# Hybrid attention of a two-layer network: heads handled in pairs instead of one by one

## The chip, the cores and the metric

One core of a Trainium2 chip runs the whole program. The metric is the device time of one launch in microseconds (us). The engines are TensorE (PE in the rows, its weight loads PEld), VectorE (DVE), ScalarE (ACT), GpSimd (POOL) and SyncE (SP, which issues the weight loads from memory).

## The reference, cut to what matters

Two blocks run one after the other on a sequence of 256 tokens of width 1024: first a retention layer, a feed-forward, a stick-breaking attention and a mixture of experts, then two layers of a hybrid mixer, each followed by a feed-forward with a convolution. The change lies in the hybrid mixer. Half its width is attention with 8 heads of 64; the three dilated windows act together as one bias over all 256 keys:

```python
q = apply_rotary(heads(aq, ATTN_HEADS))
k = apply_rotary(heads(ak, ATTN_HEADS))
v = heads(av, ATTN_HEADS)
attn = dilated_attention(q, k, v)
...
h_fwd = mlstm_direction(q, k, v, g[0], jax.nn.log_sigmoid(g[1]))
...
mlstm = (hm * mlstm_head_g.astype(f32) * jax.nn.sigmoid(mo.astype(f32))).astype(hn.dtype)
return jnp.concatenate([attn, mlstm], axis=-1) @ w_out
```

The other half is a gated recurrence with 4 heads of 128, forwards and backwards, whose q and k come out of a convolution over 5 tokens and a silu.

## The kernel before, in words

All weights come as units of 128x2048 floats through a ring of buffers (`Stream`). `advance` (L101) splits what has arrived into a high part on ScalarE (`split_h`, L83) and a low part on VectorE (`split_l`, L94), so that a product takes three matmuls of reduced precision. The order of instructions in the program is the order on each engine; nothing reorders them, and a late instruction holds up all behind it on its engine.

`hybrid` walks over 14 units of input weights; unit u ends with an `advance`. Units 0 to 3 give q and k of attention, in halves. `rotated` (L1008) applies the rotation on VectorE into a tile `ro`, `flip` (L1020) turns that tile on TensorE and ScalarE copies it to `qk`. The flip of unit u-1 stands right behind the matmuls of unit u. In unit 3 `gating` (L970) runs a chain of small operations on VectorE. Units 5, 6, 9 and 10 (`projA`) give q and k of the recurrence: `conv` (L1144) on ScalarE, eight `taps` (L1151) on VectorE, a tanh on ScalarE, then `silu` (L1161). Units 4 and 8 give attention's values, units 7 and 11 the recurrence's, units 12 and 13 the output gate.

Units 4 to 12 carry attention, one head a unit: `attend(n)` (L1030) turns the weights of head n-1, multiplies q and k of head n, copies the turned weights, and finds the biased maximum and the exponentials of head n. `normalise(n)` (L1059) follows behind the taps. Two units after the second head of a pair, `pv` (L1065) multiplies with the values. `todo` (L1189) sets where the recurrence stands: `gates` (L1076) computes decay tiles `Dt` (TensorE, then four exponentials on ScalarE), `mscores` (L1099) multiplies them with scores, `mout` (L1112) gives the output of one head.

PSUM has two pools: `psA` (L152), 2 slots of two banks, and `psP` (L155), 4 slots of one bank. A new tile takes the slot that the program has freed longest ago and waits until its last reader is done. `attend` takes one `psA` tile for the turned weights of one head and the scores of the next, `gates` one; each projection, flip, `pv` and `mscores` takes one `psP` tile, `mout` two.

```python
            todo = {1: [(prepare,)], 3: [(gating,)], 5: [(gates, 0)], 6: [(gates, 1)], 7: [(mscores, 0), (mscores, 1)],
                    8: [(mout, 0)], 9: [(gates, 2), (mout, 1)], 10: [(gates, 3)], 11: [(mscores, 2), (mscores, 3)],
                    12: [(mout, 2), (mout, 3)], 13: []}
```

Of the kernel before, what the change touches and what calls it, by code (L numbers as in the profile page):

```python
# [125 lines left out]
def tok(t):  # L126
    return slice(t * 128, t * 128 + 128)
# [6 lines left out]
class Net:  # L134
# [801 lines left out]
    def hybrid(self, l, joint0):  # L936
        nc, tc, a, W = self.nc, self.tc, self.a, self.W
        with tc.tile_pool(name="h1", bufs=1) as p, tc.tile_pool(name="h2", bufs=2) as w:
# [66 lines left out]
            at = p.tile([128, 4, 2, S], F32, tag="at", name="at")  # L1005
            dn = {}

            def rotated(ps):  # L1008

                x = w.tile([128, 2, 4, 2, 32], F32, tag="cv", name="ro")  # L1010
                t1, t2 = (w.tile([128, 2, 8, 32], F32, tag="wk", name=n) for n in ("t1", "t2"))
                for t, i in ((t1, 0), (t2, 1)):
                    nc.vector.tensor_tensor(t, ps.rearrange("p t (h d) -> p t h d", d=32),  # L1013
                                            cs[:, :, i, None, :].to_broadcast([128, 2, 8, 32]), op=OP.mult)
                t1, t2 = (t.rearrange("p t (h i) d -> p t h i d", i=2) for t in (t1, t2))
                nc.vector.tensor_tensor(x[:, :, :, 0, :], t1[:, :, :, 0, :], t2[:, :, :, 1, :], op=OP.subtract)
                nc.vector.tensor_tensor(x[:, :, :, 1, :], t2[:, :, :, 0, :], t1[:, :, :, 1, :], op=OP.add)
                return x.rearrange("p t h i d -> p t (h i d)")
# [8 lines left out]
                else:  # L1027
                    nc.scalar.activation(dst[0], ps, AF.Copy, scale=scale)

            def attend(n):  # L1030

                A = self.psA()
                if n > 0:
                    x = at[:, (n - 1) % 2]
                    for jt in range(2):
                        for it in range(2):
                            nc.tensor.transpose(A[:, 0, jt * S + it * 128:jt * S + it * 128 + 128], x[:, it, tok(jt)],  # L1037
                                                self.ident)
                r = slice(64 * (n % 2), 64 * (n % 2) + 64)
                ps = A[:, 1, :].rearrange("p (t s) -> p t s", t=2)  # L1040
                for t in range(2 if n < 8 else 0):
                    nc.tensor.matmul(ps[:, t, :], lhsT=qk[r, 0, n // 2, tok(t)], rhs=qk[r, 1, n // 2, :],  # L1042
                                     start=True, stop=True)
                if n > 0:
                    nc.scalar.activation(at[:, 2 + (n - 1) % 2], A[:, 0, :].rearrange("p (t s) -> p t s", t=2), AF.Copy)
                if n == 8:
                    return
                x = at[:, n % 2]
                m = self.small(2, "m")
                for t in range(2):  # L1050
                    nc.vector.tensor_tensor_reduce(x[:, t, :], ps[:, t, :], bias[:, t, :], 1.0, -3e38, op0=OP.add,  # L1051
                                                   op1=OP.max, accum_out=m[:, t:t + 1])
                nm = self.small(2, "nm")
                nc.vector.tensor_scalar(nm, m, -1.0, None, op0=OP.mult)
                dn[n] = d = self.small(2, "dn")
                for t in range(2):
                    nc.scalar.activation(x[:, t, :], x[:, t, :], AF.Exp, bias=nm[:, t:t + 1], accum_out=d[:, t:t + 1])

            def normalise(n):  # L1059
                d = dn.pop(n)  # L1060
                nc.vector.reciprocal(d, d)
                x = at[:, n % 2]
                nc.vector.tensor_tensor(x, x, d[:, :, None].to_broadcast([128, 2, S]), op=OP.mult)

            def pv(c):  # L1065
                ps = self.psP([128, S])
# [44 lines left out]

            def mout(h):  # L1112
                x = Dt.pop(h)
                A = [self.psP([128, 2, 129]) for _ in range(2)]

                def o(i, t):
                    return A[i][:, t, :]

                def vv(t):
                    return va[:, t, h, :]  # L1120

                def mm(out, l, r, start, stop):
                    nc.tensor.matmul(out, lhsT=l, rhs=r, start=start, stop=stop)  # L1123

                mm(o(0, 0), x[:, 0, 0:128], vv(0), True, True)
                mm(o(0, 1), x[:, 0, 128:256], vv(0), True, False)
                mm(o(0, 1), x[:, 0, 256:384], vv(1), False, True)
                mm(o(1, 0), x[:, 1, 0:128], vv(0), True, False)
                mm(o(1, 0), x[:, 1, 128:256], vv(1), False, True)
                mm(o(1, 1), x[:, 1, 256:384], vv(1), True, True)  # L1130
                d = self.sm.tile([128, 2, 2], F32, tag="den", name="den")
                for i in range(2):
                    nc.scalar.activation(d[:, i, :], A[i][:, :, 128], AF.Abs)
                    nc.vector.tensor_tensor(d[:, i, :], d[:, i, :], cols[:, 1, :, 32 * i + h], op=OP.max)
                r = self.sm.tile([128, 2, 2], F32, tag="rden", name="rden")
                nc.vector.reciprocal(r, d)
                for t in range(2):
                    y = mix[:, t, tok(h)]
                    nc.vector.tensor_scalar(y, o(0, t)[:, :128], r[:, 0, t:t + 1], None, op0=OP.mult)  # L1139
                    nc.vector.scalar_tensor_tensor(y, o(1, t)[:, :128], r[:, 1, t:t + 1], y, op0=OP.mult, op1=OP.add)  # L1140
                    j = w.tile([128, 128], BF, tag="junk1", name="junk1")
                    nc.scalar.activation(j, y, AF.Square, accum_out=ssq[:, 2 * h + t:2 * h + t + 1])
# [8 lines left out]
            def taps(ps, y, ks, dst):  # L1151
                for j, (o, s) in ((0, (slice(2, S), slice(0, S - 2))), (1, (slice(1, S), slice(0, S - 1))),
                                  (3, (slice(0, S - 1), slice(1, S))), (4, (slice(0, S - 2), slice(2, S)))):
                    for c, k in enumerate(ks):
                        nc.vector.scalar_tensor_tensor(y[:, c, o], ps[:, c, s], k[:, j:j + 1], y[:, c, o],  # L1155
                                                       op0=OP.mult, op1=OP.add)
                th = w.tile([128, 2, S], F32, tag="wk", name="th")
                nc.scalar.activation(th, y, AF.Tanh, scale=0.5)
                return dst, th, y

            def silu(dst, th, y):  # L1161
                nc.vector.scalar_tensor_tensor(dst, th, 1.0, y, op0=OP.add, op1=OP.mult)
# [5 lines left out]
            def mnorm():  # L1168
                nc.scalar.preload_act_table_set("sqrt_and_others")
                nc.scalar.activation(rs, ssq, AF.Sqrt, scale=4.0 / 128, bias=eps4)  # L1170
                nc.vector.reciprocal(rs, rs)
# [20 lines left out]
            for u in range(14):  # L1192
                A = u in (5, 6, 9, 10)
                ps = next(first) if u < 4 else self.projA() if A else self.projB()
                if 0 < u < 5:
                    i = u - 1
                    flip([qk[:, i % 2, i // 2 * 2:i // 2 * 2 + 2]], aq.pop(i), 0, 1.0 if i % 2 else 0.125)
                c = None
                if u < 4:
                    aq[u] = rotated(ps)  # L1200
                elif A:
                    c = conv(ps, (u - 5) % 4, u // 9)
                elif u in (4, 8):
                    i = u // 8
                    nc.scalar.activation(v[:, :, i * 256:i * 256 + 256], ps, AF.Copy)
                elif u in (7, 11):
                    i = u // 11
                    nc.scalar.activation(va[:, :, 2 * i:2 * i + 2, :128], ps.rearrange("p t (h d) -> p t h d", h=2),
                                         AF.Copy)
                else:  # L1210
                    gated(u - 12, ps)
                if u in (7, 9, 11, 13):
                    pv((u - 7) // 2)
                if u == 5:
                    columns()
                if 4 <= u < 13:
                    attend(u - 4)
                if A:
                    c = taps(*c)
                if 4 <= u < 12:  # L1220
                    normalise(u - 4)
                if A:
                    silu(*c)
                if u == 3:
                    W.advance()
                for f in todo.get(u, []):
                    f[0](*f[1:])
                if u == 4:
                    nc.scalar.preload_act_table_set("exp_and_others")
                if u not in (3, 13):  # L1230
                    W.advance()
            mnorm()
            mfinal(0)
            joint = RmsNorm(self, p, w, a["mix_post_g"][l], a["ffn_pre_g"][l], "mqk")
# [325 lines left out]
```

## Time and profile before

| what | value |
|---|---|
| median of 3 runs | 2269.43 us (2269.21 to 2270.16) |
| the profiled execution | 2271.13 us, its span 2269.3 us |
| TensorE busy (matmul) | 2209.9 us, 97% |
| TensorE busy (weight loads) | 1922.5 us, 85% |
| VectorE busy | 1705.9 us, 75% |
| ScalarE busy | 1374.1 us, 61% |
| mean granted clock of TensorE | 0.992 of full |

TensorE is busy for nearly all of the span, the other engines for less; the shares are means over phases with different limits. The two hybrid layers lie at about 1585 to 1702 us and 1930 to 2046 us. A time in a row counts from the start of the span. In a row of a timeline the first number is the start and the second the duration, "x4" counts instructions, and a bracket tells how long the engine sat idle before and what ended that.

### The profile page before, as it was taken

Reading aid. Unit: us, or ns where it says so; the run is one execution under the profiler, and the core shown is the slowest. Engines: PE = TensorE matmul, PEld = TensorE weight load, DVE = VectorE, ACT = ScalarE, POOL = GpSimd, SP = SyncE. Lnnn points to the kernel's source line nnn. Section 1 sums busy time; section 2 is a strip of 40 time slices with the busy share of each in tenths; the row PEclk is TensorE's granted clock in tenths of the full one; section 3 lists DMA queues with packets and bytes.
Section 4 is the critical chain, followed back from the end, with each engine's and each line's share of the span. In section 5 each row is a group of like instructions: output and inputs, shape, how many; then the busy total and the mean of one; then the engine's idle time right before and its main releaser. Section 6 shows DMA issues by size and latency. Waiting matters only on the chain. (4 is left out here: it accounts for less than half of the span.)

```text
span 2269.3 us, 31847 instructions
## 1 busy us (share of the span) xinstructions
PE 2209.9 (97%) x13077; PEld 1922.5 (85%) x13077; DVE 1705.9 (75%) x1671; ACT 1374.1 (61%) x1380; POOL 63.4 (3%) x78
## 2 busy tenths in 40 slices
PE   8999999998999999999999999997999999999998
PEld 8998998987888888878887888886889998888996
DVE  6566554647889888888888888887876975776972
ACT  4353543664777777777776777775556654555752
POOL 4100000010000000000000000000000000000000
PEclk9999999999999999999999999998999999999999
DMA  8444555537988899989998999995234554434551
GB/s 305 163 170 173 200 186 184 174 129 279 397 328 311 303 386 366 352 309 376 355 351 301 345 377 366 353 345 185 94 131 169 205 186 167 151 130 143 204 192 68
DMA packets 80074, 562.07 MB, mean 248 GB/s; under 512 B 9072, under 2 KB 9136, under 8 KB 13488
## 3 DMA queue, kind: packets, MB, share of 16 engines
q1 hardware_dynamic: 76464, 547.39, 65.7%
q0 software_dynamic: 3456, 12.55, 1.7%
q8 instruction: 105, 1.72, 0.3%
q14 instruction: 49, 0.40, 0.0%
HBM read 558.86 MB, written 1.05 MB: 247 GB/s over the span
## 5 line engine op out<-in xcount | busy, mean ns | idle before, releaser
L94 DVE TENSOR_TENSOR wl<-raw,wh 128x2048 fp32r<-128x2048 f32 x518 | 1185.3, 2291 | 318.8 <-ACT wh L83 316.7
L83 ACT ACTIVATE wh<-raw 128x2048 fp32r<-128x2048 f32 x518 | 991.2, 1915 | 393.7 <-PE pp L754 198.7
L200 PE MATMUL pp<-xh,wh 128*128 128x256 f32 x1360 | 389.0, 286 | 7.5 <-ACT wh L194 7.4
L200 PE MATMUL pp<-xh,wl 128*128 128x256 f32 x1360 | 385.6, 283 | 0.1
L200 PE MATMUL pp<-xl,wh 128*128 128x256 f32 x1360 | 384.3, 283 | 0.0
L200 PEld LDWEIGHTS pp<-xh,wh 128*128 128x128 f32 x1360 | 257.0, 189 | 9.3 <-ACT wh L194 8.1
L200 PEld LDWEIGHTS pp<-xl,wh 128*128 128x128 f32 x1360 | 258.8, 190 | 0.5 <-issue 0.5
L200 PEld LDWEIGHTS pp<-xh,wl 128*128 128x128 f32 x1360 | 257.7, 189 | 1.2 <-DVE wl L195 0.9
L200 PE MATMUL pp<-wh,xh 128*128 128x256 f32 x720 | 206.8, 287 | 5.2 <-DVE mix L1139 5.2
L200 PE MATMUL pp<-wh,xl 128*128 128x256 f32 x720 | 203.1, 282 | 0.0
L200 PE MATMUL pp<-wl,xh 128*128 128x256 f32 x720 | 202.6, 281 | 0.0
L754 PE MATMUL pp<-wh,xgh 128*128 128x512 f32 x448 | 179.5, 401 | 3.8 <-DVEq L831 3.8
L754 PE MATMUL pp<-wh,xh 128*128 128x512 f32 x448 | 179.4, 400 | 0.0
L754 PE MATMUL pp<-wl,xgh 128*128 128x512 f32 x448 | 177.2, 396 | 1.5 <-DVE wl L94 1.5
L754 PE MATMUL pp<-wl,xh 128*128 128x512 f32 x448 | 177.7, 397 | 0.7 <-DVE wl L94 0.7
L754 PE MATMUL pp<-wh,xl 128*128 128x512 f32 x448 | 177.6, 396 | 0.0
L754 PE MATMUL pp<-wh,xgl 128*128 128x512 f32 x448 | 177.0, 395 | 0.0
L200 PEld LDWEIGHTS pp<-wh,xh 128*128 128x128 f32 x720 | 136.6, 190 | 7.9 <-issue 6.1
L764 PE MATMUL pa<-wh,hh 128*128 128x512 f32 x448 | 142.0, 398 | 0.7 <-ACT hh L194 0.7
L764 PE MATMUL pa<-wh,hl 128*128 128x512 f32 x448 | 141.4, 397 | 0.0
L764 PE MATMUL pa<-wl,hh 128*128 128x512 f32 x448 | 141.3, 397 | 0.0
L200 PEld LDWEIGHTS pp<-wl,xh 128*128 128x128 f32 x720 | 136.6, 190 | 0.9 <-issue 0.7
(335 smaller groups left out, 3054.4 us busy)
## 6 DMA issues: line engine op xcount, KB each, us to landing
raw<-in_moe_w_in SPq DMA_DIRECT2D x224, 1024.0 KB, 5.4
raw<-in_moe_w_out SPq DMA_DIRECT2D x112, 1024.0 KB, 5.5
raw<-in_w_up SPq DMA_DIRECT2D x44, 1024.0 KB, 4.8
raw<-in_w_in SPq DMA_DIRECT2D x28, 1024.0 KB, 4.8
raw<-in_ret_w_in SPq DMA_DIRECT2D x23, 1024.0 KB, 5.2
raw<-in_ffn_w_in SPq DMA_DIRECT2D x22, 1024.0 KB, 4.8
raw<-in_w_down SPq DMA_DIRECT2D x22, 1024.0 KB, 4.8
raw<-in_ffn_w_out SPq DMA_DIRECT2D x11, 1024.0 KB, 4.8
```

The source lines that it names most:

```text
L83: self.nc.scalar.activation(h, self.rt[i][0], AF.Copy)
L94: self.nc.vector.tensor_tensor(l, r, h.bitcast(F32), op=OP.subtract)
L200: self.nc.tensor.matmul(out, lhsT=w, rhs=x, start=(i == 0), stop=(i == n - 1))
L754: nc.tensor.matmul(q, lhsT=x[:, k, :], rhs=ww[:, kk, :], start=(k == 0 and i == 0), stop=(k == KC - 1 and i == 2))
L764: nc.tensor.matmul(A[0][f], lhsT=x[:, k, :], rhs=ww[:, kk, half(f)], start=(s == 0 and k == 0 and i == 0), stop=(s == SL - 1 and k == 3 an ...
```

## The change

`attend` is split into `scores(c)` and `turn()`, and both work on a pair of heads. In units 4, 6, 8 and 10 `scores` multiplies q and k of both heads, one in rows 0 to 63 and one in rows 64 to 127 of the array, in turn, and finds maxima and exponentials of both; `normalise` handles the pair in one go and moves behind the unit's `advance`. In units 6, 8, 10 and 12 `turn` turns the pair's weights of two units before, ahead of the new scores, with one copy of 128x1024. `pv` stays in units 7, 9, 11 and 13, a unit behind the turn. The flips of q and k move back by one unit; so that no tile is overwritten, the first two rotated tiles lie in `sg`. `mout(2)` takes a `psA` tile instead of two `psP` tiles. `silu` follows the taps at once.

```diff
-            def attend(n):
...
+            def scores(c):
+                A = self.psA().rearrange("p j (t s) -> p j t s", t=2)
+                for t in range(2):
+                    for j in range(2):
+                        r = slice(64 * j, 64 * j + 64)
+                        nc.tensor.matmul(A[:, j, t, :], lhsT=qk[r, 0, c, tok(t)], rhs=qk[r, 1, c, :],
+                                         start=True, stop=True)
+                m = self.small(4, "m")
...
+                for i in range(4):
+                    x = at[:, i // 2, i % 2, :]
+                    nc.scalar.activation(x, x, AF.Exp, bias=nm[:, i:i + 1], accum_out=d[:, i:i + 1])
+            def normalise(c):
+                d = dn.pop(c)
+                nc.vector.reciprocal(d, d)
+                x = at[:, :2].rearrange("p j t s -> p (j t) s")
+                nc.vector.tensor_tensor(x, x, d[:, :, None].to_broadcast([128, 4, S]), op=OP.mult)
+            def turn():
+                A = self.psA().rearrange("p j (t s) -> p j t s", t=2)
+                for j in range(2):
                     for jt in range(2):
                         for it in range(2):
+                            nc.tensor.transpose(A[:, j, jt, tok(it)], at[:, j, it, tok(jt)], self.ident)
+                nc.scalar.activation(at[:, 2:], A, AF.Copy)
...
             def mout(h):
                 x = Dt.pop(h)
-                A = [self.psP([128, 2, 129]) for _ in range(2)]
+                if h == 2:
+                    wide = self.psA()
+                    A = [wide[:, i, :258].rearrange("p (t c) -> p t c", t=2) for i in range(2)]
+                else:
+                    A = [self.psP([128, 2, 129]) for _ in range(2)]
...
-                if 0 < u < 5:
-                    i = u - 1
+                if 1 < u < 6:
+                    i = u - 2
...
-                if 4 <= u < 13:
-                    attend(u - 4)
+                if u in (6, 8, 10, 12):
+                    turn()
+                head = {4: 0, 6: 1, 8: 2, 10: 3}.get(u)
+                if head is not None:
+                    scores(head)
                 if A:
-                    c = taps(*c)
-                if 4 <= u < 12:
-                    normalise(u - 4)
-                if A:
-                    silu(*c)
+                    silu(*taps(*c))
...
                 if u not in (3, 13):
                     W.advance()
+                if head is not None:
+                    normalise(head)
```

Three places show how instructions move; all are of the second hybrid layer.

On VectorE in units 4 and 5, before: the negated maxima of head 0, its normalise, unit 4's weight split, the columns of the gates, and the first maximum of head 1.

```order
L1054 TENSOR_SCALAR nm<-m 128x2
L1061 RECIPROCAL dn<-dn 128x2
L1063 TENSOR_TENSOR at<-at,dn 128x512
L94 TENSOR_TENSOR wl<-raw,wh 128x2048
L1003 COPY gcols<-pp 128x144
L1051 ISA at,m<-pa,con 128x256
```

Now, with the four maxima of pair 0 ahead of it:

```order
L1046 TENSOR_SCALAR nm<-m 128x4
L94 TENSOR_TENSOR wl<-raw,wh 128x2048
L1054 RECIPROCAL dn<-dn 128x4
L1056 TENSOR_TENSOR at<-at,dn 128x1024
L1003 COPY gcols<-pp 128x144
L1160 SCALAR_TENSOR_TENSOR cv<-pp,lay,cv 128x254 x2
```

The normalise has moved behind the weight split, has twice the width, and stands ahead of the taps of unit 5.

On ScalarE from the exponentials of unit 4 to the first copy of turned weights in unit 6, before:

```order
L1057 ACTIVATE at,dn<-at,nm 128x256 x2
L1229 ACT_TABLE_LOAD
L83 ACTIVATE wh<-raw 128x2048
L1148 ACTIVATE cv<-pp,lay 128x256 x2
L1045 ACTIVATE at<-pa 128x512
L1057 ACTIVATE at,dn<-at,nm 128x256 x2
L1158 ACTIVATE th<-cv 128x512
L1096 ACTIVATE Dt<-pa,gcols 128x256
L1096 ACTIVATE Dt<-pa,gcols 128x128 x2
L1096 ACTIVATE Dt<-pa,gcols 128x256
L83 ACTIVATE wh<-raw 128x2048
L1148 ACTIVATE cv<-pp,lay 128x256 x2
```

Now:

```order
L1050 ACTIVATE at,dn<-at,nm 128x256 x4
L1233 ACT_TABLE_LOAD
L83 ACTIVATE wh<-raw 128x2048
L1029 ACTIVATE qk<-pp 128x512
L1153 ACTIVATE cv<-pp,lay 128x256 x2
L1163 ACTIVATE th<-cv 128x512
L1097 ACTIVATE Dt<-pa,gcols 128x256
L1097 ACTIVATE Dt<-pa,gcols 128x128 x2
L1097 ACTIVATE Dt<-pa,gcols 128x256
L83 ACTIVATE wh<-raw 128x2048
L1153 ACTIVATE cv<-pp,lay 128x256 x2
L1064 ACTIVATE at<-pa 128x1024
```

Four exponentials of `at` stand ahead of the table load instead of two, unit 5 has none and no copy, and the last flip's copy to `qk` has moved into it. The copy of the turned pair comes behind the gate exponentials (`Dt`), the weight split and the conv of unit 6.

On TensorE in unit 6, between the projections of units 6 and 7, before (the first three rows of `gates(1)` are the last rows here):

```order
L1037 MATMUL pa<-ident,at 128x128 x4
L1042 MATMUL pa<-qk 128x256 x2
L1085 MATMUL pa<-M,con 128x256
L1085 MATMUL pa<-M,con 128x128 x2
L1085 MATMUL pa<-M,con 128x256
```

Now:

```order
L1063 MATMUL pa<-ident,at 128x128 x8
L1037 MATMUL pa<-qk 128x256 x4
L1086 MATMUL pa<-M,con 128x256
L1086 MATMUL pa<-M,con 128x128 x2
L1086 MATMUL pa<-M,con 128x256
```

The turn of pair 0, the scores of pair 1 and `gates(1)` each take a tile of `psA`, where one tile served the first two.

## Rows read from the trace of the kernel before

**Rows 1.** Waits of TensorE, second hybrid layer: engine, tile, line, releaser, total us, times, longest.
```profile
PE pp L200 <- DVE mix L1139: 2.6, 1, 2.6
PE pa L1037 <- DVE at L1063: 2.5, 3, 1.6
...
PE pp L1024 <- DVE ro L1017: 2.0, 2, 1.3
```

**Rows 2.** Waits of TensorE, first hybrid layer (1585 to 1702 us).
```profile
PE pp L1024 <- DVE ro L1017: 4.3, 2, 3.0
...
PE pa L1037 <- DVE at L1063: 1.1, 1, 1.1
```

**Rows 3.** Timeline of VectorE: start, us, line, operation, tiles.
```profile
1616.31 0.42 DVE L1051 CUSTOM_DVE_ANT_0 at<-pa,con 128x256 f32<-128x256 f32 x1
...
1958.80 0.42 DVE L1051 CUSTOM_DVE_ANT_0 at<-pa,con 128x256 f32<-128x256 f32 x1
...
1961.40 0.69 DVE L1063 TENSOR_TENSOR at<-at,dn 128x512 f32<-128x512 f32 x1
...
1964.42 2.29 DVE L94 TENSOR_TENSOR wl<-raw,wh 128x2048 fp32r<-128x2048 f32 x1 [2.33 <-ACT wh L83]
...
1967.73 3.20 DVE L1155 SCALAR_TENSOR_TENSOR cv<-pp,lay,cv 128x254 f32<-128x254 f32 x8
```

**Rows 4.** Stretches: busy us and count by engine, TensorE clock, DMA share, GB/s.
```profile
1934.70:1953.00 18.30, 16.29 (x138) 15.90 (x137) 18.15 (x23) 9.76 (x9) 2.46 (x3) 1.00 0.66 230
1604.70:1608.20 3.50, 3.50 (x19) 3.50 (x18) 3.47 (x6) 1.71 (x1) 0.00 (x0) 0.51 0.67 215
1694.70:1698.10 3.40, 3.40 (x29) 3.40 (x30) 1.93 (x8) 1.55 (x10) 0.00 (x0) 1.00 0.54 227
2038.10:2041.70 3.60, 3.60 (x20) 3.60 (x19) 1.53 (x6) 2.10 (x5) 0.00 (x0) 0.53 0.25 107
```

**Rows 5.** Timeline of ScalarE, second hybrid layer.
```profile
1960.57 0.50 ACT L1057 ACTIVATE at<-at,nm 128x256 f32<-128x256 f32 x1
...
1961.18 1.28 ACT L1229 ACT_TABLE_LOAD   x1
...
1971.02 0.63 ACT L1158 ACTIVATE th<-cv 128x512 f32<-128x512 f32 x1 [2.07 <-DVE dn L1061]
...
1971.56 1.33 ACT L1096 ACTIVATE Dt<-pa,gcols 128x256 f32<-128x256 f32 x4
...
1974.57 1.04 ACT L1148 ACTIVATE cv<-pp,lay 128x256 f32<-128x256 f32 x2
...
2010.38 0.25 ACT L1133 ACTIVATE den<-pp 128x2 f32<-128x2 f32 x2
...
2012.95 1.90 ACT L83 ACTIVATE wh<-raw 128x2048 fp32r<-128x2048 f32 x1
```

**Rows 6.** Groups of ScalarE by line, second hybrid layer: busy us, mean ns.
```profile
L1394 ACT ACTIVATE junk<-pa 128x1024 bf16<-128x1024 f32 x1 | 1.0, 1023 | 1.9 <-PE pa L239 1.9
```

**Rows 7.** Timeline of TensorE's matmuls in five places.
```profile
437.14 0.71 PE L489 MATMUL pa<-qT,kT 64*128 64x256 f32 x4
...
1633.16 0.36 PE L200 MATMUL pp<-wh,xh 128*128 128x256 f32 x1
...
1973.49 0.93 PE L1085 MATMUL pa<-M,con 4*128 4x256 f32 x8
...
1974.56 0.37 PE L200 MATMUL pp<-wh,xh 128*128 128x256 f32 x1
...
1991.20 0.60 PE L1037 MATMUL pa<-ident,at 128*128 128x128 f32 x4
1991.72 1.13 PE L1042 MATMUL pa<-qk 64*128 64x256 f32 x4
...
2012.56 0.93 PE L1085 MATMUL pa<-M,con 4*128 4x256 f32 x8
...
2037.14 0.36 PE L200 MATMUL pp<-wh,xh 128*128 128x256 f32 x1 [2.58 <-DVE mix L1139]
```

More of the change, by code (lines that the diff above doesn't have):

```diff
@@ L1006, in hybrid, with rotated @@
             dn = {}
-            def rotated(ps):
-                x = w.tile([128, 2, 4, 2, 32], F32, tag="cv", name="ro")
+            def rotated(ps, n):
+                x = sg[:, n, :] if n < 2 else w.tile([128, 512], F32, tag="cv", name="ro")
+                x = x.rearrange("p (t h i d) -> p t h i d", t=2, h=4, i=2)
                 t1, t2 = (w.tile([128, 2, 8, 32], F32, tag="wk", name=n) for n in ("t1", "t2"))
@@ L1028, in flip @@
                     nc.scalar.activation(dst[0], ps, AF.Copy, scale=scale)
-            def attend(n):
-                A = self.psA()
-                if n > 0:
-                    x = at[:, (n - 1) % 2]
+            def scores(c):
[7 more added lines that the diff above has]
+                for j in range(2):
+                    for t in range(2):
+                        nc.vector.tensor_tensor_reduce(at[:, j, t, :], A[:, j, t, :], bias[:, t, :], 1.0, -3e38,
+                                                       op0=OP.add, op1=OP.max,
+                                                       accum_out=m[:, 2 * j + t:2 * j + t + 1])
+                nm = self.small(4, "nm")
+                nc.vector.tensor_scalar(nm, m, -1.0, None, op0=OP.mult)
+                dn[c] = d = self.small(4, "dn")
+                for i in range(4):
+                    x = at[:, i // 2, i % 2, :]
+                    nc.scalar.activation(x, x, AF.Exp, bias=nm[:, i:i + 1], accum_out=d[:, i:i + 1])
@@ L1035, in attend @@
+            def normalise(c):
[5 more added lines that the diff above has]
+                A = self.psA().rearrange("p j (t s) -> p j t s", t=2)
+                for j in range(2):
                     for jt in range(2):
                         for it in range(2):
-                            nc.tensor.transpose(A[:, 0, jt * S + it * 128:jt * S + it * 128 + 128], x[:, it, tok(jt)],
-                                                self.ident)
@@ L1039, in attend @@
[L1039 to L1063, printed above, removed]
+                            nc.tensor.transpose(A[:, j, jt, tok(it)], at[:, j, it, tok(jt)], self.ident)
+                nc.scalar.activation(at[:, 2:], A, AF.Copy)
             def pv(c):
@@ L1199, in hybrid @@
                 if u < 4:
-                    aq[u] = rotated(ps)
+                    aq[u] = rotated(ps, u)
                 elif A:
```

## The prediction, made before the changed kernel ran

> **What bounds the kernel now.** TensorE is busy for nearly the whole span, so I first asked where it is not: the table of waits of the two hybrid layers. The reader is to see three waits there: for the rotated tile `ro`, for the normalised tile `at`, and for `mix`, which frees the PSUM slots that unit 13 needs: 2.0, 2.5 and 2.6 us in the second layer [rows 1], and 4.3 and 1.1 us in the first, where the row for `mix` reads the same [rows 2]. The change is aimed at all three. The second question is whether TensorE could run ahead if they were gone. The timeline of VectorE has the first masked maximum of attention, the instruction behind the gating chain, at 1616.31 and at 1958.80 us [rows 3]; I call this moment T. In the 18.30 us from the first rotation of the second layer to that chain, VectorE is busy for 18.15 [rows 4]. Its queue, not TensorE, sets T, and the change adds and removes nothing in that queue ahead of T. So T stays, however early TensorE comes. The third view is the clock of TensorE by stretches: after the long wait for `ro` and after the wait for `mix` in the second layer it stands near half, 1.2 GHz, and after the same wait in the first layer it stays at 2.4 [rows 4].
>
> **Edits that cost or give nothing by themselves.** The rotated tiles move into `sg`, and the flips come one unit later: the waits for `ro` go, 2.0 and 4.3 us, but they lie before T, and what TensorE gains there it must give back at its next wait for VectorE. Two small reciprocals and negations in each pair go too, under half a us of VectorE. The order of weight loads on SP is the same, row for row, so no transfer moves.
>
> **Step 1: unit 6, from T on.** The order rows show what is queued. Four masked maxima come at 0.42 each with some 0.2 to the exponentials [rows 3], then four exponentials at 0.50 [rows 5] where there were two: the table load starts at T+3.9. From table load to VectorE's weight split takes 3.24 (1961.18 to 1964.42) [rows 3, 5], so T+7.1. From that split to the taps 3.31 pass, of which two maxima, 0.84, are gone from this place; in come the normalise, now behind the split, and for two heads, 2 times 0.69 [rows 3]: 2.5 and 1.4, so the taps start at T+11.0, and the turn on TensorE no earlier. Tanh comes 3.29 after the taps' start, the gate exponentials 0.54 later, and they take 1.33 [rows 3, 5]: T+16.2. They read the PSUM tile that the scores of pair 1 need, since `psA` has two slots and unit 6 now takes three tiles; before, this moment was T+14.1, and only `gates(1)` came behind it. So the scores of pair 1 start at T+16.2. The other slot holds the turn, and `gates(1)` waits for ScalarE to copy it. From the gate exponentials' start (T+14.8) to the next conv is 3.01, the conv takes 1.04 [rows 5], and a copy of 128x1024 out of PSUM 1.02, by the one activation of that size [rows 6]: `gates(1)` at T+19.9. The projection of unit 7 follows 1.07 later, as from 1973.49 to 1974.56 [rows 7]: T+21.0. That is 1979.8 where it was 1974.56, and 1637.3 where it was 1633.16 [rows 7]: **5.2 and 4.1 us later**, although TensorE had nothing to wait for up to unit 5.
>
> **Step 2: from there to the projection of unit 13**, 62.58 us in the second layer now (1974.56 to 2037.14) [rows 7]. Gone: the heads of units 7, 9 and 11, each 0.52 from transposes to scores and 1.13 of scores [rows 7], 5.0 in all. Gone: the waits behind unit 7's start, 2.0 of the 2.5 (the first of the three lies before it) and 2.6 in the second layer, 1.1 and 2.6 in the first [rows 1, 2]. Added: four transposes more in units 8, 10 and 12, 0.52 each, 1.5. The scores of a pair cost TensorE no more than those of one head did: two row halves that stand together take 0.71 for four instructions in the first block, against 1.13 for four in one half [rows 7], so eight should take about 1.13. I take that; not overlapped they would take 2.26.
>
> **The new wait in step 2.** From the scores of unit 8 a chain runs to the tile that `gates(3)` needs in unit 10: scores 1.13, maxima 1.9, exponentials 2.0, the first output's denominators to the next weight split on ScalarE 2.57 (2010.38 to 2012.95) [rows 5], 1.95 to VectorE's split (3.24 less the table load's 1.28), that split 2.29, a normalise 1.4, taps to tanh 3.29, 0.54, gate exponentials 1.33, the second output's 2.57, 1.7 to the conv (3.01 less 1.33), 1.04, and the copy 1.02: 24.7 us. TensorE's own work between these points took 20.84 without a wait (1991.72 to 2012.56) [rows 7], less the head of unit 9, 1.65, plus 0.5 of transposes: 19.7. So it waits 5.0 in units 9 and 10: part for the slot of the values' product, whose low part now stands behind a normalise, the rest for the turn's copy. Nothing here was a wait before, so its lower bound is 0; the upper, with a copy as slow as two of 0.63, 5.3. I take 5.0, since each term has a row.
>
> The sum of steps 1 and 2: second layer 5.2 - 5.0 - 4.6 + 1.5 + 5.0 = +2.1; first 4.1 - 5.0 - 3.7 + 1.5 + 5.0 = +1.9. **Together 4.0 us slower.** Behind unit 13 nothing changes: the table load and the root that follow hang on that unit's end.
>
> **Step 3: the clock.** In a stretch at the low level 20 matmuls start in 3.60 us; at full clock 29 start in 3.40 [rows 4], so 20 take 2.3: a drop costs 1.3. The one behind unit 12 of the second layer goes with its wait: -1.3. The one of the first layer lies before T and was covered by VectorE. The new pauses in unit 6 are over 4 us (T+12.0, the turn's end, to T+16.2) and 2.6, with 1.1 of work between; those of units 9 and 10 make 5.0 in two parts. Of the three old pauses of this length, two were followed by a drop. I count one drop behind each unit 6 and one for the two units 10: 3 times 1.3 = 3.9. The bounds are none and four with each lasting twice as long, 10.4. The Trainium skill ("TensorE: Matmul & The Clock Gate", "Loop structure matters more than you think") says that a loop which leaves TensorE waiting between its bursts sends the clock down to half. By that rule each of the four pauses would be followed by a drop, and the sum would be 1.3 higher; the row of the first layer's last wait, at clock 1.00 behind it, is one pause that was not.
>
> **The sum**: 4.0 - 1.3 + 3.9 = +6.6. The profiled execution took 2271.13 (its span is 2269.3), 1.7 above the median of 2269.43; on that median the forecast is **2276.0 us**. A measurement of this kernel can tell about 0.2%, 4.5 us, from no change.
>
> **Rivals.**
> *The waits are shorter and the clock holds.* If half of step 2's wait is hidden (5.0 less over both layers) and no drop follows, the sum is 4.0 - 5.0 - 1.3 = -2.3: 2267. For it: no wait stood there before, and one long pause had no drop. Against: each link stands in one engine's queue in the order rows. Chance 0.22; it lies within 0.2%.
> *TensorE's savings count in full, and the kernel is faster.* The mechanism is in unit 6: if the gate exponentials and the turn's copy are done before TensorE arrives there, nothing is given back. Then all waits go, 7.1 and 8.0, four score blocks of 1.13 in each layer, 9.0, and the drop, 1.3: 2244; half of it, 2257. It decides at step 1's +5.2: VectorE would have to reach T, or the taps, some 5 us sooner, and the only idle time ahead of T is 0.15 us in 18.30 [rows 4]. Chance 0.15 with all cases between.
> *The row halves do not run together, so that the change does not do what it says.* Then each pair takes 1.1 more, but in units 4, 6 and 10 behind waits; only unit 8 pays: +2.2, 2278. It lies within the forecast's own range, with 0.05 of its chance.
>
> **How the numbers follow.** The forecast has 0.63, with its own range from 2274 (two drops fewer) to 2285 (drops twice as long). The first rival reaches down to 2266; below it stands the second, most of whose 0.15 is left out, and a little above 2285. So the range is 2266 to 2285, and the chances are 0.15 faster, 0.22 within 0.2%, 0.63 slower.
>
> **What would show it.** Right: no wait for `ro` and none for `mix` in unit 13; in unit 6 three waits, for VectorE's normalise, for ScalarE's `Dt` and for its copy to `at`, some 4 us the longest; a wait for `yl` before the projection of unit 10 and one for the copy before `gates(3)`; T as far behind the first rotation as now; scores of a pair in about 1.1 us; the clock low in unit 7. Wrong: a projection of unit 7 that starts by T+17, or the projection of unit 13 nearer to T than now, 78.3 us (1958.80 to 2037.14).

## The result, and the profile after

The change makes the kernel slower: 2282.86 us against 2269.36 (medians of six runs each), a ratio of 1.0058 with a 95% interval of 1.0046 to 1.0069, 13.5 us. Forecast were 2276.0, in a range of 2266 to 2285. The direction is right, the loss is twice as large as forecast. The span of the profiled execution is 2282.2 us (2269.3 before), the mean granted clock 0.981 (0.992).

The waits of TensorE, second hybrid layer, in place of [rows 1]; columns as there:

```profile
PE pa L1086 <- ACT at L1064: 4.8, 2, 3.3
PE pa L1037 <- ACT Dt L1097: 3.9, 1, 3.9
PE pa L1063 <- DVE at L1056: 2.1, 1, 2.1
PE pp L200 <- DVE yl L195: 1.3, 1, 1.3
```

The waits for `ro`, for the old `at` and for `mix` are gone, 7.1 us. In their place stand 12.1 us for the copy of the turned pair, the gate exponentials, the normalise and `yl`. The first layer has the same ones (4.8, 4.1, 0.9 and 1.3) and one more, 1.5 in unit 5 for the last flip's copy to `qk`.

Timeline of TensorE from the first scores of the second layer to unit 13, where [rows 7] stood before:

```profile
1960.52 1.13 PE L1037 MATMUL pa<-qk 64*128 64x256 f32 x8
...
1977.47 1.27 PE L1063 MATMUL pa<-ident,at 128*128 128x128 f32 x8 [2.06 <-DVE at L1056]
...
1982.68 2.08 PE L1037 MATMUL pa<-qk 64*128 64x256 f32 x8 [3.94 <-ACT Dt L1097]
...
1986.30 1.66 PE L1086 MATMUL pa<-M,con 4*128 4x256 f32 x8 [1.54 <-ACT at L1064]
...
1988.25 0.56 PE L200 MATMUL pp<-wh,xh 128*128 128x256 f32 x1
...
2018.52 0.39 PE L200 MATMUL pp<-xh,wh 128*128 128x256 f32 x1 [1.34 <-DVE yl L195]
...
2029.76 1.66 PE L1086 MATMUL pa<-M,con 4*128 4x256 f32 x8 [3.28 <-ACT at L1064]
...
2031.71 0.56 PE L200 MATMUL pp<-wh,xh 128*128 128x256 f32 x1
...
2051.58 0.36 PE L200 MATMUL pp<-wh,xh 128*128 128x256 f32 x1
```

The rows are the scores of pair 0, the turn, the scores of pair 1, `gates(1)` and the projection of unit 7, then the projection of unit 10, `gates(3)`, and the projections of units 11 and 13. The eight scores of pair 0 take 1.13, no more than four did in [rows 7]: the row halves run together. Those of pair 1, behind a wait of 3.94, take 2.08, and `gates(1)` reaches its projection in 1.95 (1986.30 to 1988.25) where it took 1.07 (1973.49 to 1974.56).

VectorE in the same layer, in place of [rows 3]: the first rotation, the first masked maximum (T), the weight split, the normalise of the pair, the taps of unit 5.

```profile
1942.72 1.28 DVE L1014 TENSOR_TENSOR t<-pp,rot 128x512 f32<-128x512 f32 x2
...
1966.64 0.42 DVE L1042 CUSTOM_DVE_ANT_0 at<-pa,con 128x256 f32<-128x256 f32 x1
...
1973.69 2.29 DVE L94 TENSOR_TENSOR wl<-raw,wh 128x2048 fp32r<-128x2048 f32 x1 [5.37 <-ACT wh L83]
...
1976.10 1.23 DVE L1056 TENSOR_TENSOR at<-at,dn 128x1024 f32<-128x1024 f32 x1
...
1977.46 3.20 DVE L1160 SCALAR_TENSOR_TENSOR cv<-pp,lay,cv 128x254 f32<-128x254 f32 x8
```

T lies 23.9 behind the first rotation (24.1 before), although nothing waits for `ro` any more. Then VectorE is idle for 5.37, and the normalise stands behind that hole instead of in it.

ScalarE, in place of [rows 5]: gate exponentials, conv, copy of the turned pair.

```profile
1981.29 1.33 ACT L1097 ACTIVATE Dt<-pa,gcols 128x256 f32<-128x256 f32 x4
...
1984.30 1.03 ACT L1153 ACTIVATE cv<-pp,lay 128x256 f32<-128x256 f32 x2
1985.20 1.05 ACT L1064 ACTIVATE at<-pa 128x1024 f32<-128x1024 f32 x1
```

TensorE by stretches, in place of [rows 4], columns as there. The first four are the low parts of the projections of units 7 and 11 (first layer, then second), the fifth unit 13 of the second layer, the sixth the whole low stretch from unit 6 into unit 7 of the second layer, the seventh the one from unit 10 into unit 11, the last one in unit 5 of the first layer:

```profile
1638.40:1643.60 5.20, 5.20 (x27) 5.20 (x25) 3.86 (x10) 4.02 (x14) 0.00 (x0) 0.50 0.47 186
1682.40:1688.00 5.60, 5.60 (x29) 5.60 (x27) 4.21 (x12) 4.03 (x14) 0.00 (x0) 0.50 0.47 174
1988.30:1991.80 3.50, 3.50 (x18) 3.50 (x17) 3.14 (x9) 2.34 (x9) 0.00 (x0) 0.50 0.68 272
2031.70:2036.20 4.50, 4.50 (x24) 4.50 (x22) 3.75 (x10) 3.29 (x12) 0.00 (x0) 0.50 0.51 217
2051.60:2055.00 3.40, 3.40 (x31) 3.40 (x31) 2.52 (x11) 1.29 (x8) 0.00 (x0) 1.00 0.01 2
...
1978.20:1991.70 13.50, 8.02 (x40) 6.41 (x38) 10.11 (x26) 7.73 (x18) 0.00 (x0) 0.50 0.37 140
2029.40:2036.10 6.70, 6.34 (x32) 6.02 (x33) 5.91 (x19) 3.49 (x12) 0.00 (x0) 0.50 0.44 157
...
1619.70:1623.10 3.40, 3.40 (x19) 3.40 (x18) 0.00 (x0) 3.37 (x6) 0.00 (x0) 0.51 0.00 0
```

At full clock 31 matmuls start in 3.40 us. The 27, 29, 18 and 24 of the low parts would take 3.0, 3.2, 2.0 and 2.6; they took 2.2, 2.4, 1.5 and 1.9 more, 8.0. The gates ahead of them took 0.9 more three times and 0.5 once, 3.2. So **the low clock costs 11.2 us**, an estimate: with the 29 in 3.40 of [rows 4] as the measure it is 10.5. The low level of unit 6 stays for 13.5 us in one piece, with two pauses in it, that of unit 10 for 6.7 with the end of one pause in it; the one behind unit 12 of the kernel before lasted 3.60 [rows 4]. The stretch in unit 5 of the first layer follows the wait for `qk` and is not in this sum: behind it TensorE still waits 0.9 for VectorE's normalise, and the turn starts at T+10.8 in both layers, so it cost nothing.

| us | first layer | second layer |
|---|---|---|
| T to the projection of unit 7, before | 16.85 | 15.76 |
| the same, after (0.9 of it low clock) | 21.61 | 21.61 |
| from there to the projection of unit 13, before | 61.50 | 62.58 |
| the same, after (5.1 and 4.3 of it low clock) | 64.50 | 63.33 |
| from there to the tail, change | -0.07 | -1.57 |

Added up: 4.8 + 3.0 - 0.1 and 5.9 + 0.8 - 1.6, together 12.8 of the 12.9 by which the span grew.

### The profile page after: what moved, and what is told of

It is laid out like the page before. It is cut to its first block, busy times and chain, and to the rows that moved or that the text cites. A ratio compares the mean times of both kernels' runs of the same rounds, so it can differ in the third digit from the quotient of the medians.

```text
span 2282.2 us, 31784 instructions
## 1 busy us (share of the span) xinstructions
PE 2213.7 (97%) x13077; PEld 1929.5 (85%) x13077; DVE 1701.6 (75%) x1647; ACT 1373.3 (60%) x1372; POOL 66.7 (3%) x78
```

## Experiments

The theory: the chains in units 6 and 10 make four pauses, and most of the loss is the low clock behind them. Its rival: the chains alone set the time, whatever the clock. Times below are medians; the kernel before gave 2270.15 to 2270.51 beside these runs and 2269.36 beside the changed one, so a difference to 2282.86 carries about 1 us from that.

**The pauses filled** (`a_fill`).

```diff
-                for t in range(2):
+                for t in (0, 1) * (1, 3, 1, 4)[c]:
...
+                for _ in range(8 if u == 6 else 0):
+                    nc.tensor.transpose(A[:, 0, 0, tok(0)], self.ident, self.ident)
+                for _ in range(5 if u == 6 else 1):
```

> The changed kernel with TensorE kept at work in its pauses: the turn's transposes of unit 6 are done five times, eight transposes of the identity stand ahead of them, the scores of pair 1 are done three times and those of pair 3 four times, all into the same tile as before, so no other engine has more to do. First theory, the low clock: behind the four long pauses (units 6 and 10 of both layers) the projections of units 7 and 11 took 8.31, 8.46, 7.50 and 7.91 us where 6.0 is usual at 2.4 GHz, 8.2 us in all, and the gates ahead of each some 0.7 more, 2.8 in all. With the pauses filled the granted clock stays at 1.00 there and the time falls by 11.0, to 2271.9 (2270 to 2274). Rival, the waits themselves: the clock stays up, but what TensorE gains in units 7 and 11 it gives back at the next waits (yl ahead of the projection of unit 10, the copy ahead of gates(3)), and the time stays at 2280 to 2283.

Measured: 2271.36, a ratio to the kernel before of 1.0004 (0.9995 to 1.0013). The stretches of unit 7 in the two layers are now:

```profile
1636.40:1641.60 5.20, 5.20 (x46) 5.20 (x45) 4.41 (x14) 3.20 (x11) 0.00 (x0) 1.00 0.57 202
1979.90:1983.40 3.50, 3.50 (x33) 3.50 (x31) 3.46 (x13) 2.08 (x8) 0.00 (x0) 1.00 0.83 297
```

46 and 33 matmuls start where 27 and 18 did, and the time falls by 11.5 (12.6 if each kernel is set against the kernel before beside it), with more work on TensorE and none taken from any engine. What it gains is not given back. This settles it for the first theory: with the clock held, handling heads in pairs neither costs nor gains what a measurement of this kernel can tell.

**The turn in psP tiles** (`a_psp`).

```diff
-                A = self.psA().rearrange("p j (t s) -> p j t s", t=2)
                 for j in range(2):
+                    A = self.psP([128, 2, S])
...
-                nc.scalar.activation(at[:, 2:], A, AF.Copy)
+                    nc.scalar.activation(at[:, 2 + j], A, AF.Copy)
```

> The changed kernel with the turn in two psP tiles and two copies of 128x512, instead of one psA tile and one copy. First theory, the slots of psA: the scores of pair 1 no longer need the slot of gates(0) and start behind the turn (T+11.7 instead of T+16.0), and gates(1) needs that slot, free at T+16.0, instead of the turn's, free at T+19.7. The projection of unit 7 starts at T+17.1 instead of T+21.6, 4.5 us earlier in each layer; in unit 10 the wait of 3.3 for the copy goes. That is 15.6 in both layers, and with shorter pauses some of the 11 us of low clock: 2256 to 2267. Rival, the slots of psP: values' products and the recurrence's scores of units 7 and 11 now wait for slots that taps or copies hold, and most of it is given back: 2272 to 2283.

Measured: 2270.44. The projection of unit 7 starts at T+17.1 and T+17.6, as the first theory had it, so the slots of `psA` do set that chain. But the waits of the first layer then read:

```profile
PE pp L1103 <- DVE mqk L1167: 3.8, 2, 2.4
PE pa L1086 <- ACT Dt L1097: 2.7, 1, 2.7
...
PE pp L200 <- ACT va L1213: 1.5, 2, 0.7
PE pp L200 <- DVE yl L195: 1.3, 1, 1.3
```

So the time stays above the first theory's range and below the rival's. Some of the gain is given back, the smaller part to a slot, the one that the copy to `va` holds. The larger part goes elsewhere: the recurrence's scores wait for `mqk` itself, which VectorE makes behind four maxima and eight taps. Both theories hold in part.

**The normalise where it stood** (`a_norm`).

```diff
+                if head is not None:
+                    normalise(head)
                 if u not in (3, 13):
                     W.advance()
-                if head is not None:
-                    normalise(head)
```

> The changed kernel with the normalise of a pair ahead of the unit's advance, where it stood before the change, instead of behind it. First theory: in unit 4 VectorE is idle for 5.4 us ahead of the weight split, so there the normalise costs nothing, and taps, turn, tanh, gate exponentials and all of unit 6 come 1.4 earlier: 2.8 in both layers, 2280.1; the low clock behind the pauses stays as it is. Rival: the weight split is then held up by the exponentials of the pair, the unit behind it gets its weights later, and the time is no better than 2282.9 or worse.

Measured: 2274.85, 8.0 less, where 2.8 were expected. The projection of unit 7 starts at T+20.3 instead of T+21.6, as expected. The rest I had not counted: in unit 8 as well the normalise no longer stands between the weight split and `yl`, so the wait for `yl` goes, and the low stretches become shorter: in both layers the clock is low for some 10 us from unit 6 into unit 7 instead of 13.5, and for some 3.5 behind unit 10 instead of 6.7. How the rest divides between the two was not measured. Waits of the second layer:

```profile
PE pa L1037 <- ACT Dt L1097: 5.1, 1, 5.1
PE pa L1086 <- ACT at L1064: 4.8, 2, 3.3
```

The rival falls.

**`mout(2)` in psA, alone** (`b_mixa`, on the kernel before).

```diff
+                if h == 2:
+                    wide = self.psA()
+                    A = [wide[:, i, :258].rearrange("p (t c) -> p t c", t=2) for i in range(2)]
+                else:
-                A = [self.psP([128, 2, 129]) for _ in range(2)]
+                    A = [self.psP([128, 2, 129]) for _ in range(2)]
```

> The kernel before with one part of the change alone: mout(2) takes a psA tile instead of two psP tiles. First theory: the wait of 2.6 us for mix ahead of the projection of unit 13 goes in both layers, and the drop of the clock behind it in the second layer, 1.3: 6.5 in all, 2262.9 (2261.5 to 2264.5). Rival: the wait only moves, to the psA slot that mout(2) takes or to the tail, which needs both psA slots: 2267 to 2269.5.

Measured: 2267.53, a ratio of 0.9989 (0.9980 to 0.9998): 2.9 of the 6.5. The wait for `mix` ahead of unit 13 is gone, and this one is new in the second layer, at the flip in the tail (1.7 in the first):

```profile
PE pp L1024 <- DVE mix L1188: 1.8, 1, 1.8
```

The rest of the wait only moved behind unit 13: 6.5 less 1.8 and 1.7 is 3.0.

**`mout(2)` back in psP** (`a_mixp`, on the changed kernel, the same edit reversed).

> The changed kernel with mout(2) back in two psP tiles. First theory: the wait for mix ahead of the projection of unit 13 is back, 2.6 in each layer, nothing behind it has slack in this kernel (the tail waits for nothing), and one or two drops of the clock come with it: 2288.1 to 2290.7. Rival: the wait would have fallen into slack at the tail, where the kernel before with mout(2) in psA waited 1.8 us for mix: 2283 to 2285.

Measured: 2282.89, no change from 2282.86. That is at the lower end of the rival's range, but the wait does not fall into slack as the rival had it: most of the 2.6 does not come back at all. Only this is there, in each layer:

```profile
PE pp L200 <- DVE mix L1140: 0.6, 1, 0.6
```

What else delayed `mix` is seen on VectorE in unit 12 of the kernel before:

```profile
2029.85 0.69 DVE L1063 TENSOR_TENSOR at<-at,dn 128x512 f32<-128x512 f32 x1
2030.45 2.20 DVE L1107 SCALAR_TENSOR_TENSOR Dt<-pp,Dt 128x256 f32<-128x256 f32 x8
2032.58 2.28 DVE L94 TENSOR_TENSOR wl<-raw,wh 128x2048 fp32r<-128x2048 f32 x1
2034.77 0.68 DVE L1177 SCALAR_TENSOR_TENSOR sg<-sg,hg 128x512 f32<-128x512 f32 x1
2035.38 0.22 DVE L1134 TENSOR_TENSOR den<-den,gcols 128x2 f32<-128x2 f32 x2
```

and in this run:

```profile
2045.84 2.27 DVE L94 TENSOR_TENSOR wl<-raw,wh 128x2048 fp32r<-128x2048 f32 x1
2050.27 0.69 DVE L1178 SCALAR_TENSOR_TENSOR sg<-sg,hg 128x512 f32<-128x512 f32 x1 [2.15 <-ACT sg L1177]
2051.68 0.16 DVE L1135 TENSOR_TENSOR den<-den,gcols 128x2 f32<-128x2 f32 x1 [0.72 <-ACT den L1134]
```

Before, VectorE came to the denominators without a pause, behind a normalise, the decay products and a split. With pairs that queue is done before TensorE is there, and VectorE waits instead. The tile in `psA` is worth nothing in the changed kernel that these runs can tell.

**The flips a unit later, alone** (`b_flip`, on the kernel before).

```diff
-                if 0 < u < 5:
-                    i = u - 1
+                if 1 < u < 6:
+                    i = u - 2
...
-                    aq[u] = rotated(ps)
+                    aq[u] = rotated(ps, u)
```

> The kernel before with one other part of the change alone: the flips of q and k one unit later, the first two rotated tiles in sg. First theory, VectorE's queue sets T: the waits for ro (4.3 and 2.0 us) go, but the first masked maximum stays where it is behind the first rotation, and the time stays within 0.2% of the kernel before, 2269 to 2271. Rival: TensorE sets the pace there, and the 6.3 us come off: 2264.

Measured: 2272.62, a ratio of 1.0009 (1.0000 to 1.0018). T is 23.9 behind the first rotation of the second layer (1937.67 to 1961.58), where it was 24.1. So VectorE sets T; the waits for `ro` were slack, and TensorE waits in unit 5 instead. The time is far from the rival's 2264, but also 1.6 above the first theory's range; the last section has what the trace shows of that.

**Towards a better kernel.** The next four all have the turn in `psP` and the early normalise; the first has nothing else, the second and the third add one edit each, and the fourth adds one to the third.

> The turn in two psP tiles and the normalise ahead of the advance, together. First theory, VectorE's chain from T sets all of unit 6: it is 1.4 shorter, so the projection of unit 7 starts at T+15.7 (T+17.1 with the psP tiles alone), the wait for mqk in unit 7 stays as long since both ends move, and the wait for yl ahead of the projection of unit 10, 1.3 in each layer, goes as it did with the normalise alone: 2270.4 - 2.8 - 2.6 = 2265.0 (2263 to 2267). Rival, the gains of the two overlap: 2268 to 2271.

`a_psp_norm` has both edits and nothing else. Measured: 2265.59, a ratio of 0.9978 (0.9969 to 0.9987), as the first theory had it: the projection of unit 7 is at T+15.9 and T+15.8, and no wait for `yl` is left.

```diff
+                if A:
+                    silu(*taps(*c))
                 head = {4: 0, 6: 1, 8: 2, 10: 3}.get(u)
                 if head is not None:
                     scores(head)
-                if A:
-                    silu(*taps(*c))
```

> As the kernel with psP tiles and the early normalise, and in units 6 and 10 the taps and the silu stand ahead of the scores (behind the turn), so that VectorE makes mqk before it looks for the maxima. First theory: the silu that the recurrence's scores of units 7 and 11 wait for comes 1.6 earlier (four maxima at 0.35 and their negation), the waits for mqk (3.8 and 1.4 in all) and for va behind them go for the most part: 2265.0 - 4.5 = 2260.5 (2258 to 2263), faster than both kernels. Rival: the exponentials of the pair, now behind the tanh, hold up the normalise and the weight split behind it, and the next units wait for weights: 2264 to 2268.

`a_order`: 2285.41, 19.8 slower than without the edit, far beyond its rival. The wait for `mqk` is gone, but this one has come, 9.5 us in each layer:

```profile
PE pp L200 <- ACT va L1213: 9.5, 2, 5.0
```

ScalarE, second layer, shows what stands ahead of `va`:

```profile
1990.58 0.51 ACT L1050 ACTIVATE at<-at,nm 128x256 f32<-128x256 f32 x1 [2.34 <-DVE nm L1046]
...
1992.57 1.32 ACT L1097 ACTIVATE Dt<-pa,gcols 128x256 f32<-128x256 f32 x4
1993.78 1.91 ACT L83 ACTIVATE wh<-raw 128x2048 fp32r<-128x2048 f32 x1
1995.58 0.59 ACT L1213 ACTIVATE va<-pp 128x512 f32<-128x512 f32 x1
```

The exponentials now come behind taps and maxima, and the gate exponentials, the split and the copy to `va`, for which unit 8 waits, queue behind them. The rival had the right queue and too small a price.

```diff
                 if A:
+                    f = todo[u].pop(0)
+                    f[0](*f[1:])
                     silu(*taps(*c))
```

> The turn in two psP tiles, the normalise ahead of the advance, and in units 5, 6, 9 and 10 the gates ahead of the taps: on ScalarE the gate exponentials then stand ahead of the tanh, where ScalarE is idle (4.4 us in unit 5, 1.1 in unit 6), on TensorE nothing is put in another order. First theory, ScalarE's queue from tanh to weight split is what holds up the next unit: without the 1.33 of gate exponentials in it the weights, mqk, the copy to va and the projections of units 8 and 12 come 1.3 to 2.4 earlier in each half of a layer, and the wait of 3 us for the gate exponentials in unit 6 goes: 2265.6 less 5.2 to 9.6, 2256 to 2260.4. Rival: TensorE now waits for mqk what it waited for the gates, and a drop of the clock follows the longer wait: 2261 to 2266.

`a_gate` has this in place of the edit of `a_order`. Measured: 2261.34, a ratio of 0.9958 (0.9944 to 0.9971), 0.3 inside the rival's range. No wait for gate exponentials is left; the waits for `mqk`, which the trace puts down to the reciprocal right behind the silu, are now 4.1 and 1.4 in each layer, and a low clock follows the longer one, as the rival had it.

```profile
1978.54 2.83 PE L1103 MATMUL pp<-mqk 128*128 128x256 f32 x8 [4.11 <-DVE dn L1054]
```

```diff
-                head = {4: 0, 6: 1, 8: 2, 10: 3}.get(u)
+                head = {4: 0, 7: 1, 8: 2, 11: 3}.get(u)
```

> As the kernel with the gates ahead of the taps, and the scores of pairs 1 and 3 in units 7 and 11 instead of 6 and 10, where they stand behind the values' product and ahead of the recurrence's scores. First theory, VectorE's four maxima stand ahead of the taps of units 6 and 10 and hold up mqk: it comes 1.56 earlier, the waits for it (4.1 and 1.4) become 2.5 and 0, and without the longer one the low clock in unit 8 (6.84 instead of 5.9) goes: some 3.9 in each layer, 2261.3 - 7.8 = 2253.5 (2252 to 2257). Rival, the turn of unit 8 now comes too soon behind the scores: it waits for the exponentials and the normalise some 2 us, as does unit 12, and the time is 2258 to 2262.

`a_late`: 2258.11, a ratio of 0.9946 (0.9932 to 0.9959), **12.3 us faster than the kernel before** and 24.8 faster than the changed one; it takes in `a_gate`. It lies at the lower edge of the rival's range: the wait for `mqk` is 1.0 or less, and the turn waits for the normalise, 1.1 to 1.3 at a time:

```profile
PE pp L1063 <- DVE at L1056: 2.2, 2, 1.1
PE pp L200 <- DVE cv L1160: 1.4, 1, 1.4
```

## Why the prediction was right, and what it mis-sized

*T stays.* Right, and shown twice, by the trace after and by `b_flip`.

*Step 1.* Right to 0.2 us: taps and turn at T+10.8 (forecast 11.0), the scores of pair 1 at T+16.0 (16.2), `gates(1)` at T+19.7 (19.9). The projection of unit 7 is at T+21.6 instead of T+21.0, because `gates(1)` ran at the low clock. `a_psp` confirms the cause, the slots of `psA`.

*Step 2.* Right in the sum: without the low clock it gives -2.1 and -3.6 where -2.2 and -3.1 were forecast (the sums of 1.9 and 2.1 less step 1's 4.1 and 5.2). The new waits in units 9 and 10 are 1.3 and 3.3, 4.6 for 5.0, at the two places named. Wrong in one cause: the 2.6 for `mix` were put down to the slots; `a_mixp` shows that 2.0 of them go by the rest of the change.

*Step 3, the clock.* Here the prediction failed in size. It counted "3 times 1.3 = 3.9" and gave 10.4 as the upper bound; the low clock cost 11.2, and filling the pauses gave back 11.5. There were four places, not three, and each cost 2.8 on average. The 1.3 came from a low stretch that began 1 us behind its pause and was over in 3.60 us [rows 4]. In unit 6 two pauses follow each other with only the scores of pair 1 between, 2.08 us at the low clock, and the clock is low through both and on into the next projection; in the second layer it falls at 1978.2 already, in the turn behind the wait of 2.06. But it does not take two pauses: in unit 10 one wait of 3.3 stands before `gates(3)`, the clock is low for 6.7 us, and these places cost 2.9 and 2.8, where those of unit 6 cost 3.1 and 2.4. Why the low level lasted longer there than behind unit 12 of the kernel before stays open. The wait and the work behind it do not settle it: in `a_norm` the same 3.29 us stand ahead of the same `gates(3)` (they start at 2021.60), and the clock is low only from 2022.5 to 2025.9. The rule of the Trainium skill that the prediction weighed ("TensorE: Matmul & The Clock Gate", "Loop structure matters more than you think"), which the page shows on a long wait for a transfer, had all four pauses followed by a drop. The trace agrees with that count, at 0.50 behind each. The row set against it, one pause that left the clock at 1.00, was no guide: in `b_flip` the same wait in the first layer, again 2.6, is followed by a stretch at 0.50 (1697.0 to 1700.2).

The forecast range held the time only because its upper end, 2285, lay above the sum with the largest clock term, 2269.4 + 4.0 - 1.3 + 10.4 = 2282.5. No term stood behind that room, so at this end the range held by luck.

The refund behind unit 12 of the second layer is 1.6 for 1.3. With 11.2 for 3.9, the sum is 4.0 - 1.3 + 11.2 = 13.9, against 13.5 measured.

*Rivals.* "The waits are shorter and the clock holds" has fallen: the waits are as forecast, the clock does not hold; 2271.4 of `a_fill` is what a held clock would have given. "TensorE's savings count in full" has fallen at the point named, unit 6. "The row halves do not run together" has fallen at 1.13 us for eight.

*Still open:* besides the length of a low stretch, what in unit 12 of the changed kernel is owed to shorter queues on VectorE and what to TensorE coming later was not separated.

## What to carry to other kernels

When an engine at full load gets new pauses, price the work behind them at its low clock, and do not take the length of the low stretch from one short drop: behind the same single pause it lasted 6.7 us in the changed kernel and some 3.5 in `a_norm`; repeating harmless matmuls in the pauses shows in one run how much of a loss is clock. An instruction that moves behind a weight split or a wait takes everything queued behind it along, so the place of a normalise, of an exponential or of a tile's copy can be worth more than the instructions that a change removes. Before crediting a removed wait, ask what sets the end of that stretch: here the waits for `ro` were slack, and of the waits for `mix` with the drop behind them, 6.5 us, only 2.9 came off when they alone were removed.

## What was not expected of the hardware

The low level followed shorter pauses than those priced. In `b_flip` TensorE waits 1.65 us in unit 5 of the second layer, between small matmuls, goes on at 1.00 for 1.6 us, and then runs low for 6.7 us of unbroken work:

```profile
1965.01 0.63 PE L1038 MATMUL pa<-ident,at 128*128 128x128 f32 x4 [1.65 <-DVE at L1064]
```

```profile
1966.60:1973.30 6.70, 6.70 (x35) 6.36 (x35) 6.07 (x15) 3.54 (x9) 0.00 (x0) 0.50 0.41 143
```

35 matmuls start there where at full clock some 60 would, by the 31 in 3.40 of the changed kernel. The first layer has a low stretch of some 10 us in the same unit (1618.5 to 1628.6), with a wait of 1.5 ahead of it and the end of one of 2.0 in it. That fits that this kernel, with fewer and shorter waits ahead of T, is no faster than the one before; it was not tried apart.
